# A hybrid mixer step on one core: the memory visits written as a pipeline over all heads, adaLN sums in wider pieces

## The chip, the cores and the metric

One core of a Trainium2 chip runs the whole program. The metric is the device time of one execution in microseconds; the time given for a kernel is the median of its runs. Profiles are of one execution each.

## The reference, cut to what matters

Two layers work on 1024 latent tokens (sample) and 256 context tokens (prompt), D = 1024, all in float32. Layer AB is in question: one input projection feeds windowed attention (A) and a bidirectional matrix memory (B), and a last projection joins them. Layer C is latent attention. Shift, scale and gate of each layer (adaLN) are `silu(cond) @ w_mod[l] + b_mod[l]` for two conditions.

Branch B, for each of 4 heads of 256 channels and each of two directions, goes over the tokens chunk by chunk:

```
s   = (q @ k^T) * d_mat                       # scores within the chunk, decayed and masked
num = w_init * (q @ C) + s @ v                # C: 256 x 256 state, n: its norm
h   = num / max(|den|, exp(-m_t))
C   = w_0 * C + (k * w_s)^T @ v               # n alike
...
h = og * (h_fwd + rev(h_bwd))                 # both directions
h = h * rsqrt(mean(h*h) + EPS) * norm_w ;  b_out = h * silu(z)
```

The sample starts from a given state; the prompt starts from zero and its last state is an output.

## The kernel before, in words

Matrix products keep their precision by splitting an operand into a high and a low part (a cast on ScalarE, a difference on VectorE or GpSimd) and adding three products. All of them go through `Kern.mm` (L87), transposes through `Kern.tr` (L91), loads and stores through `Kern.dma` (L122) on SyncE's queue, a few stores through ScalarE's (L125). The order within each engine's queue is set by a planner that takes the program's order as priority and a timeline of its own for what is ready.

**Projections.** Layer AB has five projection blocks of 256 columns per memory head (`b_proj`, L1050: q, k, v, the gate o, the gate z), then keys, queries and gates for attention (`a_keys`, L777; `a_proj`, L811). A block loads its weights in four parts (`load_w`, L434: load `wf`, cast `wh`, difference `wl`) into two stage buffers and six split ones, asked for one block ahead (`Dense.stream`, L329). It then does its units of products, `proj_T` (24 matmuls of 512 or 256 columns) or `proj_N` (24 of 256), each into one PSUM bank and from there to memory.

**adaLN.** `mod_steps` (L250) forms the columns by 128: for a pair of k-tiles it loads `mw` (128 KB) and makes four products with the condition on VectorE (L284, L286, two k-tiles times two conditions) into `macc`; after eight k-tiles the sum over partitions goes through TensorE (L267), is joined with the bias (L270) and stored to `modd`. A step is taken after so many units of projections. 14 of the first 24 blocks go with head 0's projections, 10 with the memory visits, 8 more with layer C's projections (L1380). `mod_cols` (L343) reads shift and scale of layer C back and transposes them.

**Memory visits.** Chunks are of 128 tokens: eight of the sample, two of the prompt. Each chunk is visited once per direction and head, 20 visits a head, 80 in all; `step` (L1136) is one of them. The direction that comes first (`other`, ten visits in `first()`) prepares keys and scores for both and leaves scores (`sd`) and its weighted output (`st`) for the second, in memory or, where the passes meet (`turn`), on chip. The second (ten visits in `second()`) adds its own output, gates, normalises, transposes and stores to `bT`. Within a `step`, in the program's order: load the projections of the chunk (`in`, three buffers, L1144) and rows of the gates (`g`, L1147); for a first visit `prep` (L1119: key transposes to a T bank, scores to the V bank, mask L1128, exponentials L1131, product L1132, split L1133 and L1134); for a second one load `st`, `sdr`, `stz`; products with the values (L1171); split query (`qw` L1181, `qh`, `ql`) and state (`Ch` L1188, `Cl` L1189) and their products; split keys (`kwh`, `kwl`) and the state update (L1210); the divisor (L1213 to L1215). A second visit goes on at once with

```
1223  hh  = out * r + (the first visit's output)     # VectorE
1224  hh  = (tho + 1) * hh                           # VectorE, tho: half of stz
1226  ss  = sum(hh * hh)                             # ScalarE
1227  rs  = (ss / 256 + eps) ** -0.5                 # VectorE L370, GpSimd L371
1228  hh  = hh * rs                                  # ScalarE
1231  pt  = transposes of hh                         # TensorE, to a T bank
1233  sz  = pt * nb * sz ; store to bT               # VectorE, SyncE
```

PSUM's eight banks are shared here as three for the visits' products (S), two for projections (mm), one for scores (V), two for transposes (T). `weave` (L307) sets ten visits of head h beside three projection blocks of head h+1 (90 units of cost), the next ten beside two (60), the last head beside blocks of attention.

Of the kernel before, what the change touches and what calls it, by code (L numbers as in the profile page):

```python
# [19 lines left out]
D = 1024  # L20
# [56 lines left out]
class Kern:  # L77
# [64 lines left out]
def pipelined(gens, ahead):  # L142
    """the scores of a group `ahead` groups before the use of them; yields after each group"""
# [60 lines left out]
def mod_load(K, pool, k):  # L204
    """weights of the shift and the scale of the first layer for the channels of k-tile k"""
# [44 lines left out]
def mod_steps(K, p, blocks, ahead):  # L250
    """blocks (layer, first column) of 128 columns of the adaLN projection for both conditions: the products on the
    vector engine, the sum over the partitions on the tensor engine; yields after the products of two k-tiles"""
    nc = K.nc
    parts = [(l, f, k) for l, f in blocks for k in range(0, KD, 2)]
    asked = []

    def ask():
        if parts:
            l, f, k = parts.pop(0)
            w = K.t(p, [128, 2, 128], F32, "mw", ahead)  # L260
            K.dma(w, K.I["w_mod"][l, k * 128:(k + 2) * 128, f:f + 128].rearrange("(k p) f -> p k f", p=128))
            asked.append(w)

    def total(l, f, acc):
        ps = K.ps()
        for cd in range(2):
            K.mm(ps[0:2, 0:128], K.sel[cd], acc[:, cd], cd == 0, cd == 1)  # L267
        bm = K.t(p, [2, 128], F32, "bmod", 2)
        K.dma(bm, K.I["b_mod"][l:l + 1, f:f + 128].to_broadcast([2, 128]))
        nc.vector.scalar_tensor_tensor(bm, ps[0:2, 0:128], 0.5, bm, ALU.mult, ALU.add)  # L270
        K.dma(K.modd[l][:, f:f + 128], bm)
# [4 lines left out]
    for l, f in blocks:  # L276
        acc = K.t(p, [128, 2, 128], F32, "macc", 2)
        for k in range(0, KD, 2):
            w = asked.pop(0)
            for i in range(2):  # L280
                for cd in range(2):
                    c = K.condT[:, cd * KD + k + i:cd * KD + k + i + 1]
                    if k + i == 0:
                        nc.vector.tensor_scalar(acc[:, cd], w[:, i], c, None, ALU.mult)  # L284
                    else:
                        nc.vector.scalar_tensor_tensor(acc[:, cd], w[:, i], c, acc[:, cd], ALU.mult, ALU.add)  # L286
            ask()
            if late and k == 6:
                late()
            yield  # L290
        late = partial(total, l, f, acc)
    late()
# [14 lines left out]
def weave(main, n, side, total, lag=0):  # L307
    """n steps of main, and side (which costs total) spread over them, `lag` steps later"""
# [46 lines left out]
def gate_rows(K, p, l):  # L355
    """the gates of both conditions on all partitions"""
# [35 lines left out]
def xT_tile(K, x, xT):  # L392
    """the normalised tokens of a tile transposed"""
# [40 lines left out]
def load_w(K, wp, src, cols, bufs=8, width=256, kt=2):  # L434
    """weights [1024, F] in parts of kt k-tiles, split into hi and lo"""
# [61 lines left out]
def split_out(K, pool, src, P, N, scale, dh, dl, eng=None):  # L497
    """hi and lo parts of src to memory"""
# [3 lines left out]
    l = K.t(pool, [128, 512], F32R, "so_l", 2)[0:P, 0:N]  # L502
# [27 lines left out]
def layer_ab(K):  # L530
# [35 lines left out]
    mods = [(0, 2 * D + f) for f in range(0, D, 128)] + [(1, f) for f in range(0, 2 * D, 128)]  # L566
# [45 lines left out]
    dense.mods = mod_steps(K, mp, mods[:14], 4)  # L612
# [28 lines left out]
    weave(ml[3].first(), 10, dense.stream(2), 60)  # L641
    weave(ml[3].second(), 10, dense.stream(2), 2*30)
# [7 lines left out]
    def beside(n):  # L650
        """the dense blocks, the first n groups of products with more banks than later"""
# [59 lines left out]
def load_wout(K, p, src, ks):  # L711
    """the k-tiles ks of the rows, split"""
# [11 lines left out]
def out_tile(K, p, srcs, wt, gate, res, nk, each=None, xb=1, fast=False):  # L724
    """residual + gate * (tokens of one tile times wt); srcs: per part (dram, k0, k1, ...) of the transposed input"""
# [51 lines left out]
def a_keys(K, wt):  # L777
    nc, I, d, tp, rtab = K.nc, K.I, K.d, K.tp, K.rtab
    for j in range(2):
        for ci, (t0, N) in enumerate(CHUNKS):  # L780
            ps = proj_T(K, wt, j * 128, ci)
            if ci < 2:
                src = rope(K, tp, ps, 128, t0, N, rtab, ROT16)
                split_out(K, tp, src[:, 0:N], 128, N, 0.125, d["kh"][j][:, t0:t0 + N], d["kl"][j][:, t0:t0 + N])
            else:
                kr = K.t(tp, [128, 512], F32, "rp_s", 2)[:, 0:256]
                nc.vector.tensor_copy(kr, ps[:, 0:256])
                split_out(K, tp, kr, 128, 256, 0.125, d["kh"][j][:, 1280:1536], d["kl"][j][:, 1280:1536])
# [981 lines left out]
```

## Time and profile before

| | |
|---|---|
| runs | 2770.95, 2778.02, 2782.99 us |
| median | 2778.02 us |
| the profiled execution: its span from the first to the last instruction | 2769.7 us |
| TensorE busy | 2616.6 us, 94% of the span |
| mean granted TensorE clock | 0.982 |
| VectorE, ScalarE, GpSimd busy | 1812.0, 1389.3, 1095.5 us |
| moved by DMA | 351.4 MB, 127 GB/s |

The time of the profiled execution beside its span is not shown; the span is what the profile adds up to. Up to 70 us the first tokens and the first adaLN columns are made; projections and gates go on to 265 us; the visits with their projections fill 265 to 1100 us; attention, the last projection and the start of layer C go on to about 1960 us; layer C's attention and the output follow. "Waits" are idle time of an engine right before an instruction, put down to what came last. An idle engine off the path costs nothing by itself. A matmul's busy time is modelled.

### The profile page before, as it was taken

To read this page: it belongs to the slowest core of one execution; us is meant where nothing else is said; L and a number is where in the kernel's file an instruction comes from. 1 tells how busy PE (TensorE), PEld (TensorE's weight loads), DVE (VectorE), ACT (ScalarE), POOL (GpSimd) and SP (SyncE) were. 2 spreads that over 40 slices of the span, in tenths; PEclk is the share of its full clock that TensorE was granted. 3 is DMA by queue.
4 is the path that set the end of the run, shared out by engine and by line. 5 is a ranking of instruction groups with operands and counts; after the bars stand their busy time and mean duration, and the time that the engine had idled before them with its cause. 6 is when DMAs were issued, how large, how long until landed. Compare 5 with 4: busy or idle time off the path is not lost. (4 is left out here: it accounts for less than half of the span.)

```text
span 2769.7 us, 47832 instructions
## 1 busy us (share of the span) xinstructions
PE 2616.6 (94%) x16295; PEld 2283.1 (82%) x16295; DVE 1812.0 (65%) x4257; ACT 1389.3 (50%) x3382; POOL 1095.5 (40%) x1383
## 2 busy tenths in 40 slices
PE   8899998988998998999899999999899999999998
PEld 6788897887897887788778888898689999999887
DVE  7884764664653664656575655535788888888853
ACT  5222533442443442555574443331488888888842
POOL 4232422332332332434263335331464555555742
PEclk9999999999999999999999999999999999999999
DMA  7445666656666757333454237423510111110333
GB/s 243 135 131 159 168 185 178 160 173 177 165 176 170 235 182 176 96 109 109 139 156 140 86 104 237 164 61 101 158 34 30 40 30 36 36 30 22 118 100 126
DMA packets 350358, 351.38 MB, mean 127 GB/s; under 512 B 31233, under 2 KB 291070, under 8 KB 349858
## 3 DMA queue, kind: packets, MB, share of 16 engines
q1 hardware_dynamic: 344354, 343.08, 42.0%
q10 hardware_dynamic: 5760, 5.25, 0.8%
q8 instruction: 129, 2.11, 0.3%
q14 instruction: 115, 0.94, 0.1%
HBM read 236.66 MB, written 111.56 MB: 126 GB/s over the span
## 5 line engine op out<-in xcount | busy, mean ns | idle before, releaser
L448 POOL TENSOR_TENSOR wl<-wf,wh 128x512 fp32r<-128x512 f32 (+2 forms) x144 | 223.3, 1560 | 290.6 <-ACT wh L447 208.4
L87 PE MATMUL mm<-hTh,wh 128*128 128x512 f32 (+1 forms) x832 | 306.9, 369 | 8.3 <-DVE sz_th L526 3.5
L87 PE MATMUL mm<-hTl,wh 128*128 128x512 f32 (+1 forms) x832 | 304.6, 366 | 0.0
L87 PE MATMUL mm<-hTh,wl 128*128 128x512 f32 (+1 forms) x832 | 303.5, 365 | 0.3 <-POOL wl L448 0.3
L87 PE MATMUL S<-cK,cQ 96*128 96x512 f32 (+3 forms) x1248 | 298.0, 364 | 3.8 <-ACT cPb L1672 2.0
L1720 DVE TENSOR_TENSOR cpl<-T,cph 128x512 fp32r<-128x512 f32 x336 | 228.1, 684 | 41.7 <-ACT cph L1719 38.1
L87 PEld LDWEIGHTS S<-cK,cQ 96*128 96x128 f32 (+1 forms) x1248 | 191.9, 189 | 27.3 <-ACT cPb L1672 5.1
L1719 ACT CAST cph<-T 128x512 fp32r<-128x512 f32 x336 | 192.5, 590 | 34.0 <-PE T L91 22.4
L888 POOL TENSOR_SCALAR att_p<-att_p,att_den 128x640 f32<-128x640 f32 (+2 forms) x160 | 118.6, 755 | 191.2 <-DVE att_den L885 180.2
L87 PEld LDWEIGHTS mm<-hTh,wh 128*128 128x128 f32 x832 | 160.7, 193 | 31.0 <-DVE sz_th L526 4.2
L1670 DVE TENSOR_REDUCE cmx<-S 128x1 f32<-128x512 f32 x256 | 173.0, 681 | 16.3 <-PE S L87 14.0
L87 PEld LDWEIGHTS mm<-hTh,wl 128*128 128x128 f32 x832 | 160.8, 193 | 24.8 <-POOL wl L448 1.2
L87 PEld LDWEIGHTS mm<-hTl,wh 128*128 128x128 f32 x832 | 160.9, 193 | 21.3
L87 PE MATMUL V<-cph,cV 128*128 128x256 f32 x672 | 177.1, 290 | 0.0
L87 PE MATMUL V<-cpl,cV 128*128 128x256 f32 x672 | 172.2, 285 | 0.2 <-DVE cpl L1720 0.2
L447 ACT CAST wh<-wf 128x512 fp32r<-128x512 f32 (+2 forms) x144 | 89.2, 626 | 157.9 <-DMA wf<-in_w_in_ab 111.2
L883 ACT ACTIVATE att_p<-D,att_nm 128x641 f32<-128x641 f32 (+2 forms) x160 | 114.0, 715 | 98.5 <-DVE att_nm L882 57.4
L286 DVE SCALAR_TENSOR_TENSOR macc<-mw,condT,macc 128x128 f32<-128x128 f32 x448 | 140.3, 366 | 30.0 <-DMA mw<-in_w_mod 29.9
L1651 POOL TENSOR_SCALAR cPa<-cPa,cst 128x512 f32<-128x512 f32 x128 | 100.6, 786 | 118.3 <-DVE cst L1648 90.8
L87 PE MATMUL mm<-wh,hTh 128*128 128x256 f32 x480 | 137.2, 287 | 9.0 <-DVE vbt L1081 4.6
L902 DVE TENSOR_TENSOR att_pl<-T,att_ph 128x512 fp32r<-128x512 f32 x168 | 113.4, 686 | 43.3 <-ACT att_ph L901 41.8
L87 PE MATMUL mm<-wh,hTl 128*128 128x256 f32 x480 | 136.4, 284 | 0.0
(430 smaller groups left out, 8073.0 us busy)
## 6 DMA issues: line engine op xcount, KB each, us to landing
wf<-in_w_in_ab SPq DMA_DIRECT2D x120, 256.0 KB
in<-in SPq DMA_DIRECT2D x40, 514.0 KB
mw<-in_w_mod SPq DMA_DIRECT2D x128, 128.0 KB
st<-st SPq DMA_DIRECT2D x64, 256.0 KB
in<-in SPq DMA_DIRECT2D x32, 386.0 KB
in<-vbt SPq DMA_DIRECT2D x40, 258.0 KB
in<-cx SPq DMA_DIRECT2D x16, 640.0 KB
stz<-st SPq DMA_DIRECT2D x40, 256.0 KB
```

Source lines behind the costliest of these rows:

```text
L87: return self.nc.tensor.matmul(out, lhsT, rhs, start=start, stop=stop)
L286: nc.vector.scalar_tensor_tensor(acc[:, cd], w[:, i], c, acc[:, cd], ALU.mult, ALU.add)
L447: nc.scalar.copy(wh, wf)
L448: nc.gpsimd.tensor_sub(wl, wf, wh.bitcast(F32))
L883: nc.scalar.activation(P[:, hi, off - 128:641], S[:, off:769], AF.Exp, bias=nm[:, hi:hi + 1], accum_out=den[:, hi:hi + 1])
L888: nc.gpsimd.tensor_scalar(pv, pv, den[:, hi:hi + 1], 1.0, ALU.mult, ALU.mult)
L902: nc.vector.tensor_sub(pl, T_, ph.bitcast(F32))
L1651: nc.gpsimd.tensor_scalar(pv, pv, wt[:, c:c + 1], rd, ALU.mult, ALU.mult)
L1670: nc.vector.tensor_reduce(mx[:, b, c:c + 1], S, AX.X, ALU.max, negate=True)
L1719: nc.scalar.copy(ph, T_)
L1720: nc.vector.tensor_sub(pl, T_, ph.bitcast(F32))
```

## The change

- The 80 visits become objects of a class `Visit` with five parts, and one generator `mlstm` writes them as a pipeline over all heads: `load` (`in`, now four buffers) three visits ahead of the main part, `load_more` (`um` and `wi`, which together were `g`; `st`, `sdr`, the states) two ahead, `prep` (scores and all splits, those of the state too) one ahead, `main` (products, update, divisor, first line of the output), `normed` one behind, `tail` (transposes, gate z, the store to `bT`) two behind. It yields twice a visit, before and after `main`, so that units of projections stand between its parts. `stz` is loaded in `main`.
- The scores of `prep` go to T banks; PSUM is shared as S 3, mm 3, T 2.
- `mod_steps` takes columns by 512 (layer C: by 256), one k-tile a step: two products of that width where there were four of 128. All 24 blocks of the first group (now six) go with head 0's projections, and `mod_cols` stands before the visits.
- To make room: `split_out` can put the low part over its source or into a tile of the rotation (`over`), and `vbt` has two buffers instead of three. `hh`, `stz` and `sdr` have three instead of two.

Cut to its core (`Visit` holds the lines of `step` and `prep` in their new places; comment changes are left out):

```diff
@@ mod_steps
-    parts = [(l, f, k) for l, f in blocks for k in range(0, KD, 2)]
+    parts = [(l, f, k) for l, f in blocks for k in range(KD)]
...
-            w = K.t(p, [128, 2, 128], F32, "mw", ahead)
+            w = K.t(p, [128, width], F32, "mw", ahead)
...
-        for k in range(0, KD, 2):
+        for k in range(KD):
             w = asked.pop(0)
-            for i in range(2):
-                for cd in range(2):
...
+            for cd in range(2):
+                c = K.condT[:, cd * KD + k:cd * KD + k + 1]
+                if k == 0:
+                    nc.vector.tensor_scalar(acc[:, cd], w, c, None, ALU.mult)
+                else:
+                    nc.vector.scalar_tensor_tensor(acc[:, cd], w, c, acc[:, cd], ALU.mult, ALU.add)
@@ split_out
-    l = K.t(pool, [128, 512], F32R, "so_l", 2)[0:P, 0:N]
+    if over is None:
+        l = K.t(pool, [128, 512], F32R, "so_l", 2)[0:P, 0:N]
+    else:
+        l = src if over else K.t(pool, [128, 512], F32, "rp_t", 2)[0:P, 0:N]
@@ layer_ab
-    mods = [(0, 2 * D + f) for f in range(0, D, 128)] + [(1, f) for f in range(0, 2 * D, 128)]
+    mods = [(0, 2 * D + f) for f in range(0, D, 512)] + [(1, f) for f in range(0, 2 * D, 512)]
...
-    dense.mods = mod_steps(K, mp, mods[:14], 4)
+    dense.mods = mod_steps(K, mp, mods, 4)
...
     for _ in dense.mods:
         pass
+    mod_cols(K, 1, mp)
...
-    K.set_psum(S=3, mm=2, V=1, T=2)
+    K.set_psum(S=3, mm=3, T=2)
     bp = left("mls")
-    ml = [Mlstm(K, bp, h) for h in range(4)]
-    mp = left("mod2")
-    dense.mods = mod_steps(K, mp, mods[14:], 2)
+    ml = mlstm(K, bp)
     for h in range(3):
-        weave(ml[h].first(), 10, dense.stream(3, 8), 90)
-        weave(ml[h].second(), 10, dense.stream(2, 8), 60)
-    for _ in dense.mods:
-        pass
-    mod_cols(K, 1, mp)
-    mp.release()
+        weave(ml, 20, dense.stream(3), 90)
+        weave(ml, 20, dense.stream(2), 60)
...
-    weave(ml[3].first(), 10, dense.stream(2), 60)
-    weave(ml[3].second(), 10, dense.stream(2), 2*30)
+    weave(ml, 20, dense.stream(2), 60)
+    weave(ml, 21, dense.stream(2), 2*30)
@@ v_block
-            v = K.t(tp, [128, 2, 258], F32R, "vbt", 3)
+            v = K.t(tp, [128, 2, 258], F32R, "vbt", 2)
@@ Visit.load_more
+        if self.other:
+            self.um = K.t(bp, [128, 2, 128], F32, "um", 2)
+            K.dma(self.um, bc(d["g"][h, c, dr, 0:2], 2))
...
+        if not self.zero:
+            self.wi = K.t(bp, [128, 1, 128], F32, "wi", 2)
+            K.dma(self.wi, bc(d["g"][h, c, dr, 2:3], 1))
@@ Visit.prep
-        S = K.psV()
+            S = K.psT()
@@ Visit.main
+            if self.last:
+                K.dma(K.O["new_state_b_mem"][0, 0, dr, h].rearrange("(j p) e -> p j e", p=128), C[:, :, 0:256])
...
@@ mlstm
+    vs = [v for h in range(4) for v in visits(K, bp, h)]
+    at = lambda n, f: getattr(vs[n], f)() if 0 <= n < len(vs) else None
+    for n in range(3):
+        at(n, "load")
+    for n in range(2):
+        at(n, "load_more")
+    at(0, "prep")
+    for n in range(len(vs)):
+        at(n + 2, "load_more")
+        at(n + 1, "prep")
+        yield
+        at(n, "main")
+        at(n + 3, "load")
+        at(n - 1, "normed")
+        yield
+        at(n - 2, "tail")
...
@@ layer_c
-    dense.mods = mod_steps(K, cu, [(1, 2 * D + f) for f in range(0, D, 128)], 6)
+    dense.mods = mod_steps(K, cu, [(1, 2 * D + f) for f in range(0, D, 256)], 4, 256)
```

## Rows read from the trace of the kernel before

**Rows 1.** The page: the length of the span, and part 1, busy time of each engine with its share of the span and its instructions.

```profile
span 2769.7 us, 47832 instructions
PE 2616.6 (94%) x16295; PEld 2283.1 (82%) x16295; DVE 1812.0 (65%) x4257; ACT 1389.3 (50%) x3382; POOL 1095.5 (40%) x1383
```

**Rows 2.** Busy time by stage, the windows view: start and end of a stretch, its length, then for TensorE's matmuls, its weight loads, VectorE, ScalarE and GpSimd the busy us and (x) instructions, then mean granted clock, DMA share and GB/s. The first four are the stages in question, the last is the stretch of layer C that holds the last adaLN sums.

```profile
70.00:265.00 195.00, 182.54 (x1179) 158.54 (x1178) 144.39 (x396) 44.61 (x87) 56.76 (x46) 0.97 0.47 132
265.00:1100.00 835.00, 757.22 (x4830) 678.84 (x4829) 480.82 (x1246) 324.00 (x768) 262.35 (x310) 0.96 0.64 180
1100.00:1960.00 860.00, 834.87 (x4721) 702.05 (x4720) 495.16 (x1081) 383.17 (x831) 331.15 (x334) 0.99 0.42 127
1890.00:1960.00 70.00, 69.50 (x376) 56.25 (x375) 41.57 (x117) 17.70 (x33) 16.66 (x13) 1.00 0.37 109
```

**Rows 3.** TensorE's waits, 265 to 1100 us: the instruction that waited, what ended the wait, us in total, times, longest us.

```profile
PE T L91 <- ACT hh L1228: 38.4, 15, 5.6
PE S L87 <- ACT sd L1133: 7.2, 3, 4.2
PE mm L87 <- DVE sz_th L526: 6.6, 4, 3.1
PE mm L87 <- DVE vbt L1081: 4.6, 4, 2.2
PE mm L87 <- DVE bmod L270: 4.3, 1, 4.3
...
PE mm L87 <- ACT cpre L1061: 2.6, 1, 2.6
...
PE mm L87 <- DVE rp_s L491: 2.1, 1, 2.1
PE V L87 <- DVE g L1132: 1.7, 2, 1.0
...
```

**Rows 4.** Waits of the other engines, 265 to 1100 us (columns as in rows 3): the four on the way to the normed output.

```profile
ACT hh L1228 <- POOL hrs L371: 55.2, 28, 7.3
ACT stz L1226 <- DVE hh L1224: 54.1, 24, 10.4
...
POOL hrs L371 <- DVE hrs L370: 46.3, 18, 5.8
...
DVE hh L1224 <- DMA stz<-st: 22.2, 14, 4.0
```

**Rows 5.** TensorE's timeline, 434.2 to 438.9 us: start, us of one, instruction, out<-in, form, and in brackets the idle time before it.

```profile
434.19 0.39 PE L87 MATMUL mm<-hTl,wh 128*128 128x512 f32 x1
438.51 0.44 PE L91 MATMUL T<-small,hh 128*128 128x128 f32 x2 [3.94 <-ACT hh L1228]
```

**Rows 6.** Windows (columns as in rows 2) right behind another wait: a stretch at the lower clock and the one after it. All matmuls in both have 256 columns.

```profile
343.50:350.00 6.50, 4.94 (x23) 4.95 (x24) 6.47 (x17) 2.78 (x8) 1.15 (x5) 0.50 0.67 193
350.50:357.00 6.50, 6.50 (x57) 6.50 (x56) 4.40 (x15) 2.04 (x6) 0.93 (x2) 1.00 0.78 195
```

**Rows 7.** Windows (columns as in rows 2) of four stretches in the second passes of the four heads.

```profile
420.00:500.00 80.00, 65.58 (x353) 55.37 (x352) 35.80 (x112) 26.76 (x67) 22.41 (x25) 0.91 0.65 173
640.00:700.00 60.00, 47.59 (x265) 39.79 (x265) 24.05 (x75) 17.05 (x42) 15.24 (x17) 0.94 0.69 175
850.00:910.00 60.00, 47.50 (x252) 40.48 (x251) 22.24 (x69) 18.38 (x47) 15.85 (x19) 0.91 0.67 164
1040.00:1090.00 50.00, 39.32 (x206) 33.70 (x205) 27.73 (x77) 13.36 (x33) 15.31 (x16) 0.86 0.69 164
```

**Rows 8.** Waits of the other engines, 265 to 1100 us, once more: those that begin with a load.

```profile
POOL qw L1181 <- DMA in<-in: 137.1, 29, 13.6
POOL g L1128 <- DMA g<-grow: 122.1, 26, 10.8
...
ACT wh L447 <- DMA wf<-in_w_in_ab: 63.9, 31, 4.6
```

**Rows 9.** SyncE's queue, 265 to 1100 us, from three views: two issues of its timeline, then three of its waits, then the DMA issues of two tiles (count: shortest/median/longest ns of an issue, first and last start in us).

```profile
266.28 0.43 SPq L122 DMA_DIRECT2D C<-in_state_b_mem  x1
...
277.15 0.32 SPq L122 DMA_DIRECT2D sd<-sd  x1
...
SPq L122 <- POOL wl L448: 80.8, 49, 6.4
SPq L122 <- DMA bT<-stz: 62.2, 31, 10.1
SPq L122 <- PE S L87: 30.6, 26, 6.0
...
L122 SPq DMA_DIRECT2D g<-grow x80: 319/382/1072, 265.8 to 1047.7; - x80
L122 SPq DMA_DIRECT2D wf<-in_w_in_ab x78: 368/384/1507, 267.3 to 1094.8; - x78
```

**Rows 10.** VectorE's products of the adaLN projection from the view of groups by form (line, engine, operation, tiles, form, count | busy us, mean ns of one | idle before, and what ended it): one of 265 to 1100 us, two of 70 to 265 us, and from there a longer product of the same operation.

```profile
L286 DVE SCALAR_TENSOR_TENSOR macc<-mw,condT,macc 128x128 f32<-128x128 f32 x112 | 37.6, 370 | 24.1 <-DMA mw<-in_w_mod 24.1
...
L286 DVE SCALAR_TENSOR_TENSOR macc<-mw,condT,macc 128x128 f32<-128x128 f32 x223 | 70.2, 369 | 5.9 <-DMA mw<-in_w_mod 5.8
L284 DVE TENSOR_SCALAR macc<-mw,condT 128x128 f32<-128x128 f32 x30 | 10.5, 387 | 3.0 <-DMA mw<-in_w_mod 3.0
...
L1069 DVE SCALAR_TENSOR_TENSOR cx<-cpre,cw,cx 128x1024 f32<-128x1024 f32 x4 | 6.2, 1544 | 0.0
```

More of the change, by code (lines that the diff above doesn't have):

```diff
@@ L247, in mod_ab, with mod_steps @@
     K.A[l], K.Bm[l] = A, B
-def mod_steps(K, p, blocks, ahead):
+def mod_steps(K, p, blocks, ahead, width=512):
     nc = K.nc
-    parts = [(l, f, k) for l, f in blocks for k in range(0, KD, 2)]
+    parts = [(l, f, k) for l, f in blocks for k in range(KD)]
     asked = []
@@ L494, in rope, with split_out @@
     return t
-def split_out(K, pool, src, P, N, scale, dh, dl, eng=None):
+def split_out(K, pool, src, P, N, scale, dh, dl, eng=None, over=None):
     nc = K.nc
@@ L801, in a_keys @@
             K.tr(pt[:, a * 128:(a + 1) * 128], ck[:, a, :])
-        split_out(K, tp, pt[:, 0:256], 128, 256, 0.125, d["kh"][j][:, 1024:1280], d["kl"][j][:, 1024:1280])
+        split_out(K, tp, pt[:, 0:256], 128, 256, 0.125, d["kh"][j][:, 1024:1280], d["kl"][j][:, 1024:1280], over=False)
 def a_sinks(K, ap):
@@ L819, in q @@
                 split_out(K, K.tp, src[:, 0:N], 128, N, None,
-                          *[d[s][g][j * 128:(j + 1) * 128, t0:t0 + N] for s in ("qh", "ql")])
+                          *[d[s][g][j * 128:(j + 1) * 128, t0:t0 + N] for s in ("qh", "ql")], over=ci < 2)
                 yield 5
@@ L1172, in step @@
         K.mm(out, sh, vl, False, False)
-        zero = first and not sample
-        K.mm(out, sl, vh, False, zero)
-        key = (dr, sample)
-        if first:
-            st[key] = new_state(dr, sample)
-        C = st[key]
-        if not zero:
-            qw = K.t(bp, [128, 2, 128], F32, "qw", 2)
-            nc.gpsimd.tensor_mul(qw, qT, g[:, 2, :].unsqueeze(1).to_broadcast([128, 2, 128]))
-            qh = K.t(bp, [128, 2, 128], F32R, "qh", 2)
-            ql = K.t(bp, [128, 2, 128], F32R, "ql", 2)
-            nc.scalar.copy(qh, qw)
-            nc.vector.tensor_sub(ql, qw, qh.bitcast(F32))
-            Ch = K.t(bp, [128, 2, 258], F32R, "Ch", 2)
-            Cl = K.t(bp, [128, 2, 258], F32R, "Cl", 2)
-            nc.scalar.copy(Ch, C)
-            nc.vector.tensor_sub(Cl, C, Ch.bitcast(F32))
+        K.mm(out, sl, vh, False, self.zero)
+        C = self.st[self.key]
+        if not self.zero:
+            qh, ql, Ch, Cl = self.qh, self.ql, self.Ch, self.Cl
             for j in range(2):
@@ L1193, in step @@
                 K.mm(out, ql[:, j, :], Ch[:, j, :], False, j == 1)
-        if not (sample and last):
-            km, ws = sf[:, 0:256], cws[:, c, col:col + 1]
-            kh = K.t(bp, [128, 256], F32R, "kwh", 2)
-            kl = K.t(bp, [128, 256], F32R, "kwl", 2)
-            nc.scalar.mul(kh, km, ws)
-            nc.vector.scalar_tensor_tensor(kl, km, ws, kh.bitcast(F32), ALU.mult, ALU.subtract)
+        if self.update:
             dC = [K.psS() for _ in range(2)]
+            kh, kl = self.kh, self.kl
             for j in range(2):
@@ L1228, in step, with tail @@
         nc.scalar.mul(hh, hh, rs[:, 0:1])
+    def tail(self):
+        if self.other:
+            return
+        K, nc, h, hh = self.K, self.K.nc, self.h, self.hh
+        sz = self.sz[:, 256:512].rearrange("p (j t) -> p j t", j=2)
         pt = K.psT()
@@ L1266, in mlstm, with visits @@
-    return first, second
-class Mlstm:
-    def __init__(self, K, bp, h):
-        self.first, self.second = mlstm(K, bp, h)
+        K.dma(K.d["bT"][self.c][2 * h:2 * h + 2].rearrange("j p t -> p j t"), sz)
+def visits(K, bp, h):
+    st, kept = {}, {}
+    v = lambda *a: Visit(K, bp, h, st, kept, *a)
+    out = []
+    for i in range(4):
+        out += [v(i, 0, True, i == 0, False, True, i == 3), v(7 - i, 1, True, i == 0, False, True, i == 3)]
+        if i == 1:
+            out += [v(8, 0, False, True, False, True), v(9, 1, False, True, False, True)]
+    for i in range(4, 8):
+        out += [v(i, 0, True, False, i == 7, False, i == 4), v(7 - i, 1, True, False, i == 7, False, i == 4)]
+        if i == 5:
+            out += [v(9, 0, False, False, True, False), v(8, 1, False, False, True, False)]
+    return out
@@ new lines, in mlstm @@
+def mlstm(K, bp):
+    vs = [v for h in range(4) for v in visits(K, bp, h)]
[14 more added lines that the diff above has]
+        at(n - 2, "tail")
+    n = len(vs)
+    at(n - 1, "normed")
+    at(n - 2, "tail")
+    at(n - 1, "tail")
+    yield
```

211 lines of the change are left out of this document (106 added, 105 removed).

## The prediction

> **What bounds the kernel now.** I read the engine totals first: TensorE is busy for 94% of the span and the next engine, VectorE, for 65% [rows 1]. So a microsecond is saved only where TensorE waits, or runs at its lower clock, or has less to do; the change leaves its matmuls nearly alone. The windows by stage come next [rows 2]. The stage that the change rewrites, the memory visits woven between projections (265 to 1100 us), holds 835 us with 757.2 us of TensorE, so 77.8 us idle, at a mean granted clock of 0.96. The projections and gates before it (70 to 265) idle 12.5 us, the attention stage behind it 25.1 of 860 us.
>
> Who ends the 77.8 us is in the list of TensorE's waits [rows 3]. Half, 38.4 us in 15 waits, is one pair of transposes, those of the normed output `hh`. Then come waits for a projection bank to be emptied (`sz_th`, `vbt`, `cpre`, `rp_s`: 15.9 us) and one of 4.3 us for the bank of an adaLN sum. The rest, 77.8 - 38.4 - 15.9 - 4.3 = 19.2 us, is waits on operands of the visit, `sd` the largest with 7.2. The waits of the other engines show why `hh` is late [rows 4]: L1224 waits for the gate `stz`, the square on ScalarE for L1224, the power on GpSimd for L370, the scaling for the power. Each is a hop in a queue with other work in it, and the last hop reaches TensorE. The timeline shows what it costs there [rows 5]: from 434.2 us on TensorE stands in the middle of a projection's accumulation and waits 3.94 us for two transposes. [...]
>
> The windows of the stretches with the worst waits put 50.0 of the 77.8 us into four of them, 250 us together, all in the second passes, with DMA at 0.65 to 0.69 [rows 7].
>
> **The change, part by part.** Every sum is made against the profiled execution, whose span is 2769.7 us. What lies around the span is not shown; the lowest of the three runs is 1.3 us longer, their median 8.3 us. I subtract from the median.
>
> *Output two visits behind.* `tail` (two transposes, two products, the store to `bT`) is written after the next two visits, `normed` after the next one. A visit is 835/80 = 10.4 us, so the chain of [rows 4] gets some 20 us where it now arrives up to 5.6 us late [rows 3]. **-38.4 us.** What it holds longer, `hh` and `stz`, gets a third buffer.
>
> *Preparation one visit ahead, half a visit of projections between.* Transposes of keys, scores, masks and the splits of `C`, `q` and `k` are written before the main products of the visit ahead. Covers the 19.2 us of operand waits; the state update of the visit before the last still has to reach `Ch` and `Cl` in time, so I leave a quarter: **-14.4 us.** If that cover is short, `C` is late next, and ScalarE and VectorE queue behind the copy to `Ch`.
>
> *Loads three and two visits ahead.* GpSimd waits 137.1 us for `in` and 122.1 us for `g` now [rows 8]. TensorE is reached only through waits already counted: **0**. `g` becomes `um` and `wi`: 80 issues become 40 + 72, 32 more at 0.38 us each on SP [rows 9], 12 us on a queue with time between issues; it is covered by the two visits of lead. Without that lead it would lie in front of the weights. SP is also moved past the loads of `st`, `sdr`, the stores of `sd`, and the state stores, now right behind the last update.
>
> *Banks.* The scores move from their own bank V into the two of T, and the projections get a third. The bank waits are 15.9 us; a third bank gives one more unit of products, at least 24 matmuls of 256 columns at 6.5/57 = 0.114 us [rows 6] or 2.7 us, where the mean wait is 15.9/10 = 1.6 us and the longest 3.1. I take half, **-8.0 us**. In T, a score bank held by a late `um` would stop the next transposes. Below it is 0; above it GpSimd's 122.1 us of waits for `g` [rows 8], which the single bank V keeps from TensorE now but for 1.7 us [rows 3]. Two banks between three users are nearest to that row, and `um` now has a lead: 0, the upper end kept beside rival C.
>
> *adaLN in 512 columns.* 448 + 64 products of 128 columns become 160, of 512 columns for six blocks and 256 in layer C. All blocks of the first group now lie before the visits. Removed from the visits: 37.6 us of VectorE and the 24.1 us that it waits for `mw` [rows 10], and the bank wait of 4.3 us: **-4.3 us** on TensorE. Before the visits, 70.2 + 10.5 us go and 96 products of 512 come. No row has that width; 128 columns take 369 ns and 1024 take 1544, which puts 512 at 0.87 us, 84 us in all, bounds 0.37 and 1.54, so 35 to 148 us. VectorE has 50 us free there [rows 2]. **+3 us**, 0 to 15. The sums on TensorE move with them, the same columns in fewer matmuls: 0. 5.2 MB more in 195 us make 158 GB/s from 132, less than the 180 of the visits: 0. In layer C the products lie beside a TensorE that idles 0.5 of 70 us [rows 2]: 0. `mod_cols` reads back what was written several units of projections earlier: 0 to 3, taken 0.
>
> *In-place low parts (`over`), two `vbt` buffers.* The tile of the rotation is held until its store lands; a unit of 24 matmuls of 512 takes 48 x 0.114 = 5.5 us and there are two buffers: 0, at most some us of the `rp_s` and `vbt` kind [rows 3].
>
> *Clock.* 0.04 x 835 us is 33 us of full-rate time lost. TensorE was idle in a part of the low stretches (4.94 busy of 6.5 us in [rows 6]) and some stretches stay; I take half, **-16 us**, of 0 to 33. [...]
>
> *What comes next.* The parts above leave 77.8 - 65.1 = 12.7 us of waits. No overlapped stage here is that clean: the attention stage idles 25.1/860 = 2.9%, and 2.9% of some 760 us is 22 us. **+9.3 us.**
>
> Sum: -38.4 - 14.4 - 8.0 - 4.3 + 3 - 16 + 9.3 = -68.8, rounded to **-69 us**: 2701 us for the profile, **2709 us** for the median. A measurement of this kernel tells about 0.5% (14 us) from no change; its three runs lie 12 us apart.
>
> **Rivals.** *A: DMA takes over the second passes.* The four stretches carry 168 us of DMA time in 250 us. Take out the 50 us of waits and the clock, and the same transfers would fill over 0.9 of what is left; no stretch of [rows 7] has over 0.69. With the share stopping at 0.75 they end at 168/0.75 = 224 us, 26 us saved, and with half of the 27.8 us outside it is 40: 2738 us. For it: `in` and `wf` late even now [rows 8]. Against: loads three visits ahead spread into first passes.
>
> *B: the order written is not the order issued.* The program writes the store of `sd` before the state load of the same visit, yet SP issues `C` at 266.3 and `sd` at 277.2 [rows 9], and the transposes of [rows 5] stand inside a projection. The instructions are placed by a planner; it may have hoisted what could be hoisted, and pull the tails forward again. Then the waits change their names, and only the bank and adaLN parts stay, -8.0 - 4.3 + 3, against the +9.3: 2778 us, no change. Against: it placed the transposes too early by a chain that it took for shorter; two visits are more than that error.
>
> *C, slower: loads ahead block the weights.* SP issues in order, and it waits now up to 10.1 us for a `bT` store, 6.4 for the splits of weights, 6.0 for matmuls on S [rows 9]. A load three visits ahead waits for its buffer in front of `wf`. [...] Weights have six buffers for four parts, half a block (four units of 5.5 us and two of 2.7) or 14 us of lead; 78 parts [rows 9] are 19 blocks. Two such waits in a row (16.5 us) cost TensorE 2.5 us a block or 48 us, three (22.5 us) 8.5 or 162; between them 105 us, and 2709 + 105 = 2814 us. It decides from 4.5 us a block. Against: the longest waits of TensorE have none for weights now [rows 3], though ScalarE waits 63.9 us for `wf` [rows 8].
>
> *D: all of it.* Every wait and all of the clock: 2778 - 77.8 - 33 = 2667 us.
>
> **How the numbers follow.** Forecast 0.52, A 0.23, B 0.12, C 0.10, D 0.03. Faster by over 0.5% is forecast, A and D, 0.78; same 0.12; slower 0.10. The range goes from just above D, 2672, to 2768, short of B: it leaves out D, C and most of B, and holds the bounds of the clock and of VectorE's products (2689 to 2737).
>
> **What would show it.** Right: `hh` gone from TensorE's waits, idle under 30 us in the visit stage, its length near 770 us, a clock of 0.98 or more there, and the stage before it no longer than now. A: waits on `st`, `stz`, `in` and a DMA share near 0.75 in second passes. B: `hh` transposes still inside projections with waits. C: TensorE or GpSimd waiting on `wf` or `wl`, SP on `in` buffers. Wrong altogether if the visit stage shortens by under 20 us.

## The result, and the profile after

The changed kernel takes 2793.47 us (median of 12 runs) where the kernel before took 2782.47 beside it: a ratio of 1.0040, with a 95% interval from 1.0025 to 1.0054. It is slower by 11 us, where 2709 us, 69 less than the median then shown, had been forecast. The profiled execution took 2800.38 us. Its page, the length of the span and part 1, answers to [rows 1]:

```profile
span 2798.6 us, 47112 instructions
PE 2619.0 (94%) x16207; PEld 2288.2 (82%) x16207; DVE 1768.6 (63%) x3883; ACT 1385.3 (50%) x3382; POOL 1086.9 (39%) x1383
```

The windows by stage, with columns as in [rows 2]: the stages before, in and behind the visits, and three stretches of 20 us, one at each change from one head to the next:

```profile
70.00:274.00 204.00, 188.90 (x1172) 161.84 (x1171) 141.96 (x236) 45.14 (x87) 50.29 (x48) 0.96 0.51 147
274.00:1130.00 856.00, 750.68 (x4768) 678.16 (x4767) 454.34 (x1102) 318.44 (x767) 262.96 (x310) 0.94 0.61 170
1130.00:1990.00 860.00, 837.58 (x4716) 704.16 (x4715) 485.45 (x1013) 383.70 (x831) 329.96 (x334) 0.99 0.42 127
440.00:460.00 20.00, 11.50 (x53) 9.90 (x52) 4.04 (x13) 3.87 (x9) 4.01 (x5) 0.76 0.71 154
660.00:680.00 20.00, 9.75 (x44) 8.31 (x43) 4.04 (x13) 3.88 (x9) 4.53 (x5) 0.74 0.65 142
880.00:900.00 20.00, 10.57 (x53) 9.12 (x53) 4.04 (x13) 3.56 (x8) 3.82 (x4) 0.77 0.65 140
```

The visit stage grew from 835 to 856 us and idles 105.3 us instead of 77.8; the stage before it grew by 9; the one behind is as long as it was. The three windows at the changes of head, 60 us together, hold 28.2 us of the idle time. TensorE's waits in the stage, answering to [rows 3]:

```profile
PE S L87 <- DVE C L1229: 50.2, 12, 10.2
PE T L91 <- ACT st L1164: 11.7, 4, 5.0
PE mm L87 <- POOL wl L449: 8.5, 8, 1.5
PE T L87 <- ACT st L1164: 8.2, 2, 4.4
...
PE T L91 <- ACT hh L1255: 4.9, 1, 4.9
```

The waits for `hh` fell from 38.4 to 4.9 us and those for `sd` to 2.3, as forecast. In their place TensorE stands 50.2 us for the update of the state `C`, and 19.9 for the copy of the keys to `st`, which empties a bank of T. VectorE's, SyncE's and ScalarE's waits in the same stretch show where the update is held up:

```profile
DVE C L1145 <- DMA out_new_state_b_norm<-C: 54.1, 6, 9.6
...
DVE hh L1251 <- DMA stz<-st: 45.9, 23, 5.7
...
SPq L122 <- DMA bT<-stz: 77.6, 35, 9.0
...
SPq L122 <- DMA out_new_state_b_norm<-C: 49.4, 6, 9.8
...
ACT wh L448 <- DMA wf<-in_w_in_ab: 115.3, 32, 10.7
```

The timelines of SyncE, VectorE, ScalarE and TensorE show one of the six cases (columns as in [rows 5] and [rows 9]):

```profile
435.94 0.39 SPq L122 DMA_DIRECT2D out_new_state_b_mem<-C  x1
436.38 0.46 SPq L122 DMA_DIRECT2D out_new_state_b_norm<-C  x1
...
447.81 0.37 SPq L122 DMA_DIRECT2D C<-in_state_b_mem  x1
...
447.89 0.06 DVE L1145 MEMSET C<- 128x2 f32 x1 [9.62 <-DMA out_new_state_b_norm<-C]
...
448.79 0.42 SPq L122 DMA_DIRECT2D wf<-in_w_in_ab  x1
...
453.00 0.62 ACT L448 CAST wh<-wf 128x512 fp32r<-128x512 f32 x1 [2.95 <-DMA wf<-in_w_in_ab]
453.52 0.59 ACT L529 ACTIVATE sz_th<-mm 128x512 f32<-128x512 f32 x1
...
454.14 0.69 DVE L530 SCALAR_TENSOR_TENSOR sz_th<-sz_th,mm 128x512 f32<-128x512 f32 x1 [5.97 <-ACT sz_th L529]
...
454.82 0.47 DVE L1229 SCALAR_TENSOR_TENSOR C<-C,w0b,S 128x258 f32<-128x258 f32 x1
...
455.35 1.01 PE L87 MATMUL S<-in,sdr 128*128 128x258 f32 x3 [8.50 <-DVE C L1229]
```

At 435.9 the state of a finished prompt is sent out, in two stores. The next head's load of `C` takes over its tile and stands in SyncE's queue until the second store has landed; it is issued at 447.81, 11.4 us after that store. On VectorE a memset of two columns of the same tile stands 9.62 us for the store too. TensorE, idle from 446.85 on, waits for the update of `C` (L1229), which reads its sums out of PSUM. That update is late by two roads. It stands behind the memset on VectorE; but the memset is done at 447.95, and TensorE waits on for 7.4 of its 8.50 us. The longer road goes by SyncE's queue: the next load of `wf` is issued only behind the load of `C`, at 448.79; ScalarE casts it at 453.00 and begins to empty the bank of `sz_th` behind it; VectorE stands 5.97 us for that, and the update follows at 454.82. At the other two changes of head 9.4 of 10.25 us and 9.0 of 9.43 lie behind the memset in the same way.

In the program the store takes 256 single numbers of 4 bytes, 1 KB, no two of them side by side in `C`. The trace has 384 of 1526 packets under 512 bytes from 436 to 449 us and does not tell whose they are. That such small pieces are what takes 11.4 us is not shown. The store of the state itself, 256 KB, was issued 0.44 us ahead of it on the same queue, the DMA engines are 0.94 to 0.98 busy from 436 to 444 us, and stores of 128 KB to `bT` held SyncE for up to 9.0 us as well. A contiguous store of the same numbers was not run.

### The profile page after: what moved, and what is told of

It is laid out like the page before. It is cut to its first block, busy times and chain, and to the rows that moved or that the text cites. A ratio compares the mean times of both kernels' runs of the same rounds, so it can differ in the third digit from the quotient of the medians.

```text
span 2798.6 us, 47112 instructions
## 1 busy us (share of the span) xinstructions
PE 2619.0 (94%) x16207; PEld 2288.2 (82%) x16207; DVE 1768.6 (63%) x3883; ACT 1385.3 (50%) x3382; POOL 1086.9 (39%) x1383
## 5 line engine op out<-in xcount | busy, mean ns | idle before, releaser
L449 POOL TENSOR_TENSOR wl<-wf,wh 128x512 fp32r<-128x512 f32 (+2 forms) x144 | 216.4, 1511 | 279.1 <-ACT wh L448 175.6
L1183 POOL TENSOR_TENSOR qw<-in,wi 128x256 f32<-128x256 f32 x72 | 56.5, 785 | 267.6 <-DMA in<-in 170.0
L87 PE MATMUL mm<-wl,hTh 128*128 128x256 f32 x480 | 136.3, 284 | 7.4 <-POOL wl L449 7.3
```

The costliest lines, as they stand in the source:

```text
L87: return self.nc.tensor.matmul(out, lhsT, rhs, start=start, stop=stop)
L449: nc.gpsimd.tensor_sub(wl, wf, wh.bitcast(F32))
L1183: nc.gpsimd.tensor_mul(qw, qT, self.wi.to_broadcast([128, 2, 128]))
```

## The experiments

Each kernel was timed against the kernel before on its own chip, where that took 2762 to 2766 us. A kernel's number below is the ratio of its time to that, with its 95% interval in brackets; 0.1% is 2.8 us.

**The state tiles.** In the change and in the kernel before:

```diff
-C = ... K.t(bp, [128, 2, 258], F32, "C", 4)
+C = ... K.t(bp, [128, 2, 258], F32, "Cs" if sample else "Cp", 2)
```

> After, with the state tile C of the sample and of the prompt under names of their own, two buffers each, in place of four shared ones (the same memory). Theory 1 (the changed kernel's loss is one wait: the first visits of a new head take over the tile of a prompt state whose output store was issued a moment before, the memset on VectorE and the load queue stand until it has landed, and TensorE waits for C): the 50 us that TensorE waits for C in the visits and the low clock after them go; 2735 us, between 2715 and 2755, and no wait of TensorE for C over 10 us in sum. Rival 2 (the visits simply do not fit beside fewer products: whatever is late next takes the place): 2775 to 2795 us with other waits of TensorE of some 50 us. Rival 3 (the transposes' banks, which the scores now share, cost it): 2775 us or more, as this kernel leaves them.

> Before, with the same two pairs of state tiles. Theory 1: before the change a tile was asked for only when its visit began, behind the old head's work, and TensorE did not wait for C; 2775 to 2785 us, no change over 0.5%. Rival: the state store's landing held up the kernel before as well (its VectorE waited 23.5 us for it, three times), so this alone gains 10 to 25 us: 2757 to 2770.

The change with them: 0.9968 (0.9955 to 0.9980), 0.72% below the change, and faster than before. The memset waits no more, and of the 50.2 us 16.4 are left. The time came down by 20 us, not by the 58 between 2793 and 2735: other waits rose, TensorE's for `stz` from 6.1 to 14.9. So theory 1 names a true part and overprices it.

The kernel before gained 0.32% too (0.9968, 0.9955 to 0.9981), 8.9 us. That is just under the rival's 10 to 25 us and inside theory 1's 0.5%, but the cause is the rival's. VectorE waited for these stores in the kernel before as well (265 to 1100 us, columns as in [rows 4]):

```profile
DVE C L1116 <- DMA out_new_state_b_norm<-C: 23.5, 3, 9.2
```

So the change made this wait dearer by 0.40%, 11 us, which is all of its loss. With the tiles apart the two kernels take the same time, although the change then has the adaLN sums, which gain 1% by themselves.

**The adaLN sums alone** (the change's `mod_steps` and its place, in the kernel before).

> Before, with the adaLN sums alone changed: pieces of 512 columns (256 in the third layer), all of the second layer's before the first visit. The forecast has minus 4 and plus 3 us for it; by the two traces the stretch before the visits grew by 9 us. Theory 1: 2782 to 2790 us, the 9 us being given back in part inside the visits, which have 16 column sums fewer. Rival: the part costs nothing (2775 to 2782), the early 9 us belong to something else.

0.9896 (0.9875 to 0.9917): 29 us faster, outside both ranges. The windows rows of the visit stage, from the first visit to the first product of attention, in the kernel before and in this one, and the first of TensorE's waits in this one:

```profile
268.00:1112.00 844.00, 763.43 (x4856) 683.54 (x4854) 482.12 (x1247) 323.47 (x767) 260.77 (x309) 0.96 0.65 181
277.00:1081.00 804.00, 743.16 (x4806) 672.01 (x4805) 436.55 (x1104) 322.62 (x768) 254.38 (x309) 0.97 0.65 184
...
PE T L91 <- ACT hh L1224: 43.0, 12, 6.3
PE V L87 <- DVE g L1128: 5.2, 4, 1.8
PE mm L87 <- DVE vbt L1077: 3.9, 3, 1.7
PE S L87 <- ACT sd L1129: 2.1, 1, 2.1
PE mm L87 <- DVE sz_th L527: 1.4, 2, 1.0
```

Over these like stretches the idle time is 60.8 us against 80.6, TensorE's busy time 743.2 against 763.4, with 50 matmuls fewer and a mean clock of 0.97 against 0.96. The `hh` wait did not shrink. Those for `sd`, `sz_th`, `cpre` and `rp_s` fell or went, though the change names none of them: they come from VectorE, or from ScalarE's work that can stand behind it, and VectorE has the column products no more. Two kernels ask whether that is the place or the width:

> Before, with all adaLN sums of the second layer ahead of the first visit but in the old pieces of 128 columns (the third layer's pieces are as before too). The whole adaLN part gave 1.04% where the forecast had 1.3 us. Theory a (the gain is the place: VectorE and the load queue are free of these sums while the visits run): 0.990 to 0.994 of before. Theory b (the gain is the width, fewer and larger pieces): 1.000 to 1.006, as the stretch before the visits is then longer by more than the visits gain.

> Before, with the adaLN sums in wide pieces as in the change (512 columns ahead of the visits, 256 in the third layer), but with the last 1024 columns of the second layer's still inside the visits, in pieces of 256 with one buffer for the sums (512 does not fit there). All wide pieces ahead of the visits measured 0.9896 of before. Theory a (what counts is that VectorE has these sums out of the visits; width only makes that affordable): 0.996 to 1.001. Theory b (width alone: fewer and larger operations and loads, wherever they lie): 0.988 to 0.993.

Narrow and early: 1.0048 (1.0029 to 1.0066). Its windows, just ahead of the visits and behind:

```profile
270.00:300.00 30.00, 6.85 (x24) 1.04 (x24) 27.34 (x108) 0.00 (x0) 0.00 (x0) 0.50 0.38 109
311.00:1131.00 820.00, 757.98 (x4833) 683.75 (x4831) 437.96 (x1111) 322.09 (x767) 252.89 (x308) 0.96 0.64 181
```

VectorE is busy for 27.34 of these 30 us, TensorE has 24 matmuls in them at a granted clock of 0.50: the sums do not fit before the visits. The visits are the shorter for it, 820 us against 844. Wide but partly inside: 0.9937 (0.9915 to 0.9959), between the theories. So pieces that are wider give some 0.6%, and the place some 0.4% more, at the edge of the intervals. The split is rough: here the pieces inside have 256 columns and not 512, and two of the ten old blocks have moved ahead. What the narrow run shows plainly is that the place needs the width.

**The banks.** The first kernel puts the scores back into a bank of their own, the second does that beside the state tiles:

```diff
-K.set_psum(S=3, mm=3, T=2)
+K.set_psum(S=3, mm=2, V=1, T=2)
-            S = K.psT()
+            S = K.psV()
```

> After, with the scores of a preparation in a bank of their own again (three for sums, two for projections, one for scores, two for transposes), the pipeline otherwise as it is. Theory 1 (the state tile is the loss; the banks are a small part, the 20 us that TensorE waits for transposes' banks at most): 2775 to 2793. Rival 3 (scores in the transposes' banks are the loss): 2740 to 2760, and the wait of TensorE for C falls as well.

> After, with both the two pairs of state tiles and the scores' own bank. By the runs so far the tiles take 0.7% off the changed kernel and the bank alone nothing (1.0048 against before, where the change itself has 1.0040). Theory 1 (additive: what is left of the pipeline's loss lies in the visits' order and not in the banks): 0.996 to 0.999 of before, 2752 to 2761 us at the 2763.7 that before last took. Rival 3 (the wait for the state tile only covered the banks' effect, which shows once it is gone): 0.985 to 0.992. The tiles' kernel waits 35 us for T banks, 12 of it for the copy of the keys and 15 for the output's last product, so the rival has that to gain.

The score bank in the change: 1.0048 (1.0030 to 1.0066). Beside the state tiles: 0.9988 (0.9974 to 1.0002). Neither differs from its partner without the bank (1.0040 and 0.9968) by more than the intervals. In the first the 20 us of waits for the keys' copy went, and waits for `um`, `cpre` and `vbt` rose from 5 to 32 us. The second, called "repaired", is the base for what follows.

**The order of the visits.** First the old one, with the adaLN sums and the state tiles; then the output's transposes, products and store as a closure that the next visit calls at its head; then called behind that visit's products (`flush` calls what waits in `K.late`):

```diff
+        def tail():
             pt = K.psT()
             ...
+        K.late.append(tail)
     def step(...):
+        flush(K)
```

> Before, with the adaLN sums of the change and the two pairs of state tiles, and no pipeline. Theory 1 (two independent gains: 1.04% and 0.3%): 0.9865 of before, between 0.984 and 0.989. Rival: the tiles gain in the kernel before only because the adaLN loads crowd the same queue, so together they are worth no more than the adaLN part: 0.989 to 0.991.

> The kernel of the run above it (adaLN sums and state tiles, no pipeline), with the transposes of the normalised output and what follows them one visit later, at the head of the next visit, the rest of the order as before. It is the one step of the pipeline that the forecast had priced highest, at minus 38.4 us, by itself. Theory 1 (that price was right and the pipeline lost it elsewhere): 25 to 40 us off the kernel above, 0.972 to 0.978 of before, and TensorE's wait for the normalised output under 5 us. Rival 2 (any order of the visits waits about as much, what is late next takes its place): 0.983 to 0.989, with new waits of 25 us or more.

> The best kernel so far (adaLN sums, state tiles, transposes of the output at the head of the next visit; 0.9839 of before) with these transposes behind the next visit's products instead of ahead of them, and a third buffer for what they read. There TensorE still waits 22.4 us for the normalised output, nine times, since the chain that makes it ends behind the evictions of the products between the visits. Theory 1: that wait falls under 5 us and with it the low clock behind it, 0.974 to 0.978. Rival: what waits next (the bank of the next transposes, state updates now later in VectorE's order) takes its place, 0.981 to 0.985.

Old order with adaLN sums and state tiles: 0.9880 (0.9860 to 0.9899). Tail at the head of the next visit: 0.9839 (0.9818 to 0.9860). Tail behind its products: 0.9843 (0.9825 to 0.9862). Old order and two simple edits already beat the repaired pipeline by 1.1%. The tail one visit later gives 0.4% or 11 us, at the edge of the intervals; the forecast had 38.4 us for two visits, which was not run by itself. Some 22 us of waits for `hh` stay in nine places in both positions. The middle one is the fastest kernel of all, 2718.34 us beside 2762.08. Its banks changed to those of the change:

> The best kernel (adaLN sums, state tiles, output transposes one visit later; 0.984 of before) with the banks of the change: three for the projections, the scores among the transposes' two. The forecast priced the banks at minus 8 us. Theory 1 (right in the old order, where the waits of the products for evictions are few: 6 us of vbt and so_l): 0.981 to 0.984. Rival 3 (scores and transposes in two banks wait for each other, as the 20 us of waits for T in the changed kernel say): 0.987 to 0.991.

0.9851 (0.9833 to 0.9870), no difference. TensorE's wait for `vbt` went, and its wait for `hh` rose from 22.4 to 34.8 us. Now the pipeline's own parts, from the repaired kernel: preparation in the visit (`at(n, "prep")` right ahead of `at(n, "main")`, with `load_more` behind `main` instead of ahead of it); then one portion of products (the diff below); then both.

```diff
         at(n + 1, "prep")
-        yield
         at(n, "main")
...
-        weave(ml, 20, dense.stream(3), 90)
+        weave(ml, 10, dense.stream(3), 90)
```

> The changed kernel with both repairs (state tiles, scores' bank), with the preparation of a visit right ahead of its own products in place of a visit ahead; loads ahead and output transposes two behind as in the change, products still in two portions a visit. Theory 1b (preparing a visit ahead is what the pipeline loses by: its operations stand ahead of the visit's updates in VectorE's and ScalarE's order, so that TensorE waits for banks to be read): faster than the kernel with both repairs by 15 us or more. Rival: the preparation ahead earns the 14 us that the forecast gave it, and this kernel is slower by 10 to 20 us, with waits for the scores' split of 10 us or more.

> The changed kernel with both repairs (state tiles, scores' bank), with the products of a visit in one portion as before the change: preparation of the next visit and products of this one back to back, then all of the dense products, then the output transposes of two visits before. The repaired pipeline stands 1.1% above the kernel that has the adaLN sums and the state tiles but the old order (0.9988 against 0.988 of before). Theory 2 (the change splits the dense products in two portions a visit, so that TensorE goes twice as often from one kind of work to the other, and waits at each for banks that VectorE and ScalarE have yet to read: the sums of the projections, the scores, the states; 41 us for sz_th, vbt, cpre, um and wl in the repaired pipeline): 0.984 to 0.990 of before, and these five waits under 15 us. Rival (order within the visit, preparation and loads ahead, is what loses): 0.995 to 1.002, with the same waits.

> The changed kernel with both repairs and products in one portion, with the preparation right ahead of its own visit. In two portions this step made the repaired pipeline 0.7% slower (1.0055 against 0.9988). Theory 1c (the preparation ahead is worth what the forecast said, and more, once nothing else stands in its way): 0.994 to 0.999 of before. Rival (with all dense products between the visits, the preparation in the visit costs little or is better, as in the kernel with the old order, which stands at 0.984): 0.984 to 0.989.

Preparation in the visit: 1.0055 (1.0037 to 1.0074). One portion: 0.9913 (0.9896 to 0.9931). Both: 1.0009 (0.9995 to 1.0023). The preparation ahead, with the earlier `load_more`, earns 0.7% in two portions and 1.0% in one, so it is a good part; which share of it is the loads' was not run. The two portions cost 0.75%, and 0.46% with the preparation inside. TensorE's waits in the visits of the repaired kernel, two portions:

```profile
PE V L87 <- DVE um L1172: 12.4, 7, 3.4
...
PE mm L87 <- DVE sz_th L530: 8.1, 3, 3.5
PE mm L87 <- DVE vbt L1080: 7.2, 6, 2.4
PE mm L87 <- ACT cpre L1060: 7.0, 4, 2.2
PE mm L87 <- POOL wl L449: 6.3, 7, 1.2
```

And in one portion, with VectorE's longest wait below them:

```profile
PE mm L87 <- DVE sz_th L530: 21.0, 3, 8.5
PE mm L87 <- DVE vbt L1080: 13.6, 7, 3.0
...
DVE hh L1251 <- DMA stz<-st: 104.8, 28, 13.4
```

The time is nearly as theory 2 said (up to 0.990), its reason is not: the five waits it names (`sz_th`, `vbt`, `cpre`, `um`, `wl`) sum to 38 us here as to 41 there. Of the 14 us by which the stage is shorter, 10 are busy time of TensorE, 750.5 us after 760.7 for the same 4824 matmuls, and 4 idle time. One row did move with the portions: ScalarE's wait for `wf` falls from 77.2 us to 26.4, and with the preparation inside from 78.0 to 35.2. That this is the cause was not tested. The last row above led on. `stz` is the one load that the pipeline left in its own visit, and VectorE stands for it in front of the evictions of `sz_th` and `vbt`.

**Queue and buffers.** A third `wi` in the repaired kernel; in the one-portion kernel a third `vbt` (tail one visit behind, to make room); then instead the load of `stz` in a method of its own, one visit ahead, with the tail one visit behind again; then the same with the banks of the change:

```diff
+        at(n + 1, "load_z")
         at(n + 2, "load_more")
```

> The changed kernel with both repairs, with a third buffer for the weights of the queries (wi). In the repaired pipeline the load queue stands 130 us for the product that releases this tile (59 times), against 52 us in the kernel with the old order. Theory 3 (this holds up what stands behind it in the queue, weights and visit loads): 8 to 20 us below the repaired pipeline, 0.991 to 0.996. Rival (the queue has slack there): 0.997 to 1.000.

> The changed kernel with both repairs and products in one portion, with the third buffer of the projected values back (vbt), for which the output transposes go one visit behind in place of two and two of their tiles lose a buffer. Theory 4 (the projections' evictions stand for the stores of these values: TensorE waits 13.6 us for vbt and 21.0 for sz_th there, VectorE for the store): 0.985 to 0.988 of before, these two waits under 15 us in sum. Rival (VectorE and ScalarE are simply behind with the visit's work when the products begin, whichever buffer is asked for): 0.990 to 0.993, the wait elsewhere.

> The changed kernel with both repairs and products in one portion (0.9913 of before), with the load of the output's factors (stz) one visit ahead of the visit that reads it, instead of in it, and the output transposes one visit behind, so that three buffers do. Theory 5 (VectorE's 105 us of waits for that load, 28 times, up to 13.4 us, hold the evictions behind it, so that TensorE waits for sz_th and vbt): that wait under 30 us, sz_th and vbt under 15 us in sum, 0.983 to 0.987 of before. Rival (VectorE has slack there; TensorE's waits come from the banks and the amount of work): 0.990 to 0.994, sz_th and vbt as before.

> The run above with the banks of the change (three for the projections, scores among the transposes' two): the whole change, mended in three places (state tiles, one portion, this load ahead). Theory: with the load out of the way the third projection bank takes what is left of TensorE's waits for evictions: 0.979 to 0.984, the lowest of all. Rival 3 (scores and transposes wait for each other): 0.985 to 0.990.

A third `wi`: 0.9994 (0.9981 to 1.0008), no difference. But SyncE's wait for `qw`, which this buffer was to end, is 128.0 us after 130.5, 60 times as before, so the run does not tell what that wait costs. A third `vbt`: 0.9938 (0.9920 to 0.9957); the buffer and the nearer tail together, with one buffer less for `stz` and `hh`, gain nothing. With `stz` ahead 0.9873 (0.9853 to 0.9894), just above theory 5's range; TensorE's first waits, and VectorE's for the load:

```profile
PE T L91 <- ACT hh L1257: 13.3, 4, 5.0
PE mm L87 <- DVE vbt L1080: 12.2, 5, 3.6
...
DVE hh L1253 <- DMA stz<-st: 13.4, 6, 3.6
```

The wait for the load falls from 104.8 to 13.4 us, TensorE's for `sz_th` from 21.0 to 0.2, and the time by 0.40%, about as much as the intervals are wide. With the banks of the change 0.9929 (0.9910 to 0.9948): here they cost 0.56%, and the theory of a lowest kernel fell; the copy to `st`, in T, holds TensorE 11.6 us again.

## Why the prediction was wrong

The account, as differences of ratios: the adaLN sums alone give -1.04%, with the state tiles in the old order -1.20. The mended pipeline (state tiles, one portion, `stz` ahead, old banks) stands at -1.27, so what is left of its parts adds under 0.1%, less than the intervals. From there to the change as it is: `stz` in its visit +0.40, two portions +0.75, the banks -0.20 (no certain difference), state tiles +0.72. The forecast had -1.3 us for adaLN and -67.5 for all the rest. Measured, adaLN gives -29 us, and the rest, added to it, costs 1.44% or 40 us. So the loss is the pipeline's, and adaLN hid most of it.

What failed is the step from waits to time: the waits named were taken away, and 22 us were to be left, but three costs that the sum puts at nothing came in their place (the state tiles, the second portion and `stz`, 20, 21 and 11 us by the runs).

- **Loads ahead, 0: the step that failed first.** It saw that SyncE "is also moved past ... the state stores, now right behind the last update" and gave that no price. Two facts belong together there: the stores come earlier, and the next head's tile is asked for two visits earlier, out of the same four buffers. It costs 20 us, of which 9 were in the kernel before, in a row of VectorE's waits that the prediction did not take up. Nor did it see that `stz` is not among the loads that move.
- **Preparation ahead, -14.4.** Worth more, 0.7 to 1.0% in this order, though the old order with the preparation inside stands lower still. "Half a visit of projections between" was taken for cover alone; the second portion that it brings costs 21 us. Why is open: the waits by sum hardly change.
- **Output two visits behind, -38.4.** The wait went, to 4.9 us, and its time did not: one visit later, by itself, the tail gave 11 us. It may be that a wait of TensorE also lets VectorE and ScalarE catch up, so that once it is gone the next evictions are late; no run shows that by itself. "What comes next" had 9.3 us for that and left 22 us of waits; the trace has 105.
- **Banks, -8.0.** 0 in the old order, a loss of 0.56% in the mended one. The mechanism named, a score bank held by a late `um`, is in the trace with 2.4 us only. What holds a bank of T is the copy of the keys on ScalarE: 19.9 us, for the next transposes and for the scores. The price 0 for a full T was wrong, with another holder than the one named.
- **adaLN, -4.3 and +3.** Measured -29 us by itself. It had the rows (37.6 us of VectorE in the visits) and counted the one wait that carried the sums' name. The product of 512 columns was put at 0.87 us; here is the row, answering to [rows 10]:

```profile
L285 DVE SCALAR_TENSOR_TENSOR macc<-mw,condT,macc 128x512 f32<-128x512 f32 x84 | 65.4, 824 | 5.8 <-DMA mw<-in_w_mod 5.7
```

 So that estimate held, and the stage before the visits grew by 9 us, inside its 0 to 15. What failed is "on TensorE -4.3", in the direction that helped the total.
- **Clock, -16.** It was to rise and fell from 0.96 to 0.94 in the stage. Over the runs it went with the idle time there: 0.98 at 47.6 us idle (the fastest kernel), 0.97 at 60.8 (adaLN alone), 0.94 at 105.3. With the waits not won, this term was not either.
- **Rivals.** C, the slower one, has the right road: a load ahead that waits in SyncE's queue in front of `wf` (ScalarE's wait for `wf` rose from 63.9 to 115.3 us), and at the changes of head TensorE stops by it. It has the wrong buffer, `in` in place of a state tile with a store in flight, and another length of the road, over ScalarE's evictions and not the weights of the next products; and its 105 us are far above the 20 us that the tiles cost. B's "same" holds the measured +0.40% by number and for none of its reasons: TensorE's waits for `hh` did go. A is not seen, with DMA at 0.61 over the stage and at most 0.72 in stretches of 40 us, though VectorE's wait for `stz` rose from 22.2 to 45.9 us. That the share would stop at 0.75 was an assumption: no run shows such a stop, and from 940 to 960 us of the change it was 0.83.

## What to carry to other kernels

A load moved ahead asks for its buffer ahead too: look up who used that buffer last, and whether a store of it has only just been issued. Then look what stands behind that load in its queue, for the wait travels with it: here SyncE stood 49.4 us for such a store, and a load of `wf` behind it. Work on an engine that is not the bound one need not be free: here VectorE was busy for 65% of the span, 37.6 us of its products bore the name of 4.3 us of waits, and their removal in wide pieces was worth 29. Take one step of a pipeline at a time: here two small edits to the old order beside the adaLN sums gave more than the whole.

## What was not expected of the hardware

- A store of 1 KB, 256 single numbers in the program, right behind one of 256 KB, took 11.4 us from its issue to the release of what waited for it, and its queue and VectorE stood up to 9.8 us for such a store. Whether its neighbours or its pieces made it slow is open.
- A column product of four times the width took 2.2 times as long, 824 ns for 512 columns where 128 took 370 [rows 10]. An estimate from these two means, with time taken as linear in the width: 1.2 ns a column and some 220 ns an instruction.
